# mLSTM exponents as full-height products with zeros for the other direction, and float32r tiles moved in SBUF

## The chip, the cores and the metric

The kernel runs on one core of one Trainium2 chip. Its time is measured on the device, in microseconds (us): before the change the median of three runs is 1986.36 us, from 1985.49 to 1988.99. TensorE (PE) multiplies matrices; each product is a weight load (PEld) and a stream of the other operand, the moving one, past the loaded weights. VectorE (DVE) and ScalarE (ACT) do elementwise work, GpSimd (POOL) sets memory and does a little arithmetic, SyncE (SP) issues transfers. On-chip memory has 128 partitions; an address is a byte offset that is the same in every partition.

## The reference

Two layers (DEPTH = 2) over 512 latent and 256 context tokens of width 1024. Each layer: a modulated RMSNorm, one projection `w_in`, four mixers side by side (gated DeltaNet, windowed attention, spatial gating, bidirectional mLSTM), one projection `w_out`, then an MLP of width 4096. The part of the mLSTM that the change touches is this, for each direction, head and chunk:

```
b    = cumsum(log_sigmoid(f));  dmat[i,j] = b[i] - b[j] + ig[j]   (j <= i, else -inf)
m[i] = max(b[i] + m_prev, max_j dmat[i,j])
s    = (q k^T) * exp(dmat - m)        # the exponents
h    = (exp(b + m_prev - m) * (q C) + s v) / max(|den|, exp(-m))
```

The second direction runs over reversed tokens, and both directions' outputs are added.

## The kernel before, in words

Activations lie transposed, 128 features on the partitions and up to 768 tokens along each. A float32 product is made of three float32r products: both operands are split into a rounded high part and a rest, and `gemm` (L484) adds `whi x hhi`, `whi x hlo`, `wlo x hhi` for each of eight blocks of 128 rows. Weights come by DMA into `wst`, ACT writes the high part `whi`, DVE the rest `wlo` (`wsplit`, L456). Two halves of a weight block take turns over the buffers that `wset` lists: in the output projection and the MLP six pairs, four of them in the pool `wcp` and two in `wsp`, so that two of three gemms read their weights from `wcp`. The activations are the moving operand: 512 latent tokens and, in layer 0, also 256 context tokens, thus 24 products of 512 columns for each gemm (and 24 of 256 in layer 0). The output projection and the MLP are 72 gemms for each layer.

Pools are laid one behind the other in SBUF, and a tile's address follows from the sizes of what lies ahead of it. In the program before the change the tiles of the gemms start at these distances past a multiple of 128 bytes (rows of weights and segments of tokens are whole multiples of 512 bytes, so that every slice keeps its tile's distance):

| tile | used as | bytes past a multiple of 128 |
|---|---|---|
| `hhi`, `hlo`, `mhi`, `mlo`, `fhi`, `flo` | moving operand of all gemms | 64 |
| `whi`, `wlo` in `wsp` | weights | 64 |
| `whi`, `wlo` in `wcp`, layer 0 | weights | 32 |
| `whi`, `wlo` in `wcp`, layer 1 | weights | 96 |
| `whi`, `wlo` in the DeltaNet's `Y1`, `Nh` | weights | 32 |
| `khi`, `klo` of head pair 0, `qs` | attention scores | 32 |
| `La`, `Rm` | the mLSTM's exponents | 32, 96 |
| `ident_r`, `gmask_r`, `selP_r`, `sel2_r` | constants | 96 |

The mLSTM's exponents are made in `mlstm_weights` (L1398), for each block p of 128 tokens. Rows 0 to 15 of `La` and `Rm` belong to the forward direction, rows 32 to 47 to the backward one. One DVE instruction (L1402) writes `Rm` for both directions: minus the running maximum, copied to four heads by the mask `d4p`. Then, in a loop over the directions, a product of 16 rows `La x Rm` (tile `W`) and a bfloat16 product that adds the triangular mask (L1414, L1415), ACT's exponential, DVE's multiplication with `qks`, and the decay `qw` towards the state (`wexp`). `Rm` has two buffers.

All of this, the attention (`swa`) and four dense projections stand in one block for each layer (L1488) that is scheduled by a simulation of its instructions, so that the order on each engine is its choice. Elsewhere the order is the scheduler's too, under the waits that buffers set.

Of the kernel before, what the change touches and what calls it, by code (L numbers as in the profile page):

```python
# [9 lines left out]
F32 = mybir.dt.float32  # L10
F32R = mybir.dt.float32r
F16 = mybir.dt.float16
BF16 = mybir.dt.bfloat16
AF = mybir.ActivationFunctionType
# [7 lines left out]
NT = SEQ + CTX  # L22
# [21 lines left out]
def go(t):  # L44
# [2 lines left out]

_LAYOUT = (
    ("ident", 128), ("blk64", 128), ("triA", 128), ("triB", 128), ("fwd", 128), ("rev", 128), ("rot", 128),
    ("d4", 4), ("d4p", 4), ("nlo", 2), ("csel", 8), ("sgn", 32), ("eps", 1), ("odg", 64), ("half", 2),  # L50
    ("gmask", 128), ("up", 128), ("lw", 128), ("selP", 128), ("sel2", 256), ("lvl", 384),
    ("cos", 512), ("sin", 512),
)
# [10 lines left out]
def constants():  # L64

    c = np.zeros((128, NCONST), np.float32)

    def put(name, a):
        o, w = _OFF[name]
        c[:a.shape[0], o:o + w] = a  # L70

    p = np.arange(128)
    same = (p[:, None] // 64) == (p[None] // 64)
    le = p[:, None] <= p[None]
    ge = p[:, None] >= p[None]
    lo_half = p < 64
    put("ident", np.eye(128))
    put("blk64", same)
    put("triA", same & np.where(lo_half[None], le, ge))
    put("triB", same & np.where(lo_half[None], ge, le))  # L80
    put("fwd", le)
    put("rev", ge)
    rot = np.zeros((128, 128))
    for h in range(2):
        for i in range(32):
            rot[64 * h + 32 + i, 64 * h + i] = -1.0
            rot[64 * h + i, 64 * h + 32 + i] = 1.0
    put("rot", rot)
    t = np.arange(SEQ)
    inv = np.power(np.float32(10000.0), -np.arange(16, dtype=np.float32) / np.float32(16)).astype(np.float32)  # L90
    ang = np.concatenate([(t // 64).astype(np.float32)[:, None] * inv, (t % 64).astype(np.float32)[:, None] * inv], 1)
    ang = np.tile(ang.astype(np.float64).T, (4, 1))
    put("cos", np.cos(ang))
    put("sin", np.sin(ang))
    g = np.zeros((128, 2, 64))
    j, i = p[:, None] % 64, np.arange(64)[None]
    for s in range(2):
        d = (p[:, None] >= 64) ^ bool(s)
        ok = np.where(d, i <= j, i >= j)
        g[:, s] = np.where(ok, 0.0, NEG)  # L100
    put("gmask", g.reshape(128, 128))
    put("up", np.where(p[None] >= p[:, None], 0.0, NEG))
    put("lw", np.where(p[None] <= p[:, None], 0.0, NEG))
    r = np.arange(64)
    half, k8 = r // 32, r % 32
    live = k8 < 8
    put("selP", live[:, None] & ((p[None] >= 64) == half[:, None]))
    sel2 = np.zeros((64, 2, 128))
    for q in range(2):
        sel2[:, q] = live[:, None] & ((r[:, None] % 4) == 2 * q + (p[None] >= 64))  # L110
    put("sel2", np.tile(sel2.reshape(64, 256), (2, 1)))
    put("d4", live[:, None] & ((r[:, None] % 4) == np.arange(4)[None]))
    put("d4p", (k8 < 16)[:, None] & ((r[:, None] % 4) == np.array([0, 2, 1, 3])[None]))
    put("nlo", np.where(np.stack([k8 // 4 == 1, k8 // 4 == 3], 1), -1.0, 0.0))
    lv = [np.where((j // 2 == i // 2) & (j != i), -1.0 / 1024.0, 0.0)]
    for n in range(1, 6):
        b = 1 << n
        lv.append(((j // (2 * b) == i // (2 * b)) & (j // b != i // b)) / 1024.0)
    put("lvl", np.concatenate(lv, 1))
    cs = np.zeros((128, 8))  # L120
    for k in range(4):
        cs[32 * k, 2 * k] = cs[32 * k + 1, 2 * k + 1] = 1.0
    put("csel", cs)
    sg = np.ones((128, 32))
    sg[:, 8:16] = sg[:, 24:32] = -1.0
    put("sgn", sg)
    put("eps", np.full((128, 1), EPS))
    put("half", np.stack([lo_half, ~lo_half], 1))
    put("odg", np.where(j == i, 0.0, 1024.0))
    return c  # L130


def bc(ap, axis, n):
    shape = list(ap.shape)
    shape.insert(axis, n)
    return ap.unsqueeze(axis).to_broadcast(shape)
# [3 lines left out]
def flow_kernel(ctx, tc, t, out, dbg=None, stop=None):  # L140
    nc = tc.nc
    V, S, T, G = nc.vector, nc.scalar, nc.tensor, nc.gpsimd
# [3 lines left out]
    per = ctx.enter_context(tc.tile_pool(name="per", bufs=1))  # L146
# [5 lines left out]
    pps = ctx.enter_context(tc.tile_pool(name="pps", bufs=4, space=PSUM))  # L152
    pg = ctx.enter_context(tc.tile_pool(name="pg", bufs=1, space=PSUM))

    S.preload_act_table_set("natural_log_exp_and_others")

    def ps(name="ps", dt=F32):
# [15 lines left out]
    def mm(o, l, r, start=True, stop=True):  # L173
        T.matmul(o, lhsT=l, rhs=r, start=start, stop=stop)  # L174

    def act_(o, i, f, **kw):
        S.activation(out=o, in_=i, func=f, **kw)  # L177

    def tt(o, a, b, op, eng=None):
        (eng or V).tensor_tensor(out=o, in0=a, in1=b, op=op)  # L180

    def stt(o, a, s, b, op0, op1):
        V.scalar_tensor_tensor(out=o, in0=a, scalar=s, in1=b, op0=op0, op1=op1)  # L183

    MUL, ADD, SUB, MAX, MIN = ALU.mult, ALU.add, ALU.subtract, ALU.max, ALU.min


    crow = per.tile([16, 128], F32, name="crow")
    nc.sync.dma_start(out=crow, in_=t["crow"])

# [4 lines left out]
    def cc(name):  # L195
        o, w = _OFF[name]
        return cst[:, o:o + w]

    ident, blk64, eps, odg = cc("ident"), cc("blk64"), cc("eps"), cc("odg")
    nlo, nlo_a = (cc("nlo")[0:64, i:i + 1] for i in range(2))  # L200
    d4, d4p = cc("d4")[0:64], cc("d4p")[0:64]
    ones = const.tile([128, 128], F32, name="ones")
    V.memset(ones, 1.0)
    scT = per.tile([128, 8, 32], F32, name="scT")
# [78 lines left out]

    def layer_pools():
        lay = ctx.enter_context(ExitStack())
        return lay, lay.enter_context(tc.tile_pool(name="zp", bufs=1)), lay.enter_context(tc.tile_pool(name="ta", bufs=2))

    lay, zp, tp = layer_pools()
    ldx = ExitStack()
    ld = ldx.enter_context(tc.tile_pool(name="ld", bufs=5))  # L290

    sg = per.tile([128, 16], F32, name="csg")
    cv = per.tile([128, 16], F32, name="cv")
    pt = gi("cT")
    T.transpose(pt[:, 0:16], crow, ident[0:16, 0:16])
    V.tensor_copy(out=cv, in_=pt[:, 0:16])
# [292 lines left out]
    for l in range(DEPTH):  # L589
# [13 lines left out]
        if l:  # L603
            lay, zp, tp = layer_pools()
# [8 lines left out]
        h = modulated(l, 0, ALL, nrm, tp)  # L613
# [10 lines left out]
        o, o_k0 = gemm_pair(ahead, h, ALL, (32, 128))  # L624
        evac(zg[0:32], o, ALL, 32)
        o = ps("gatesT")
# [49 lines left out]
        for i, (which, j) in enumerate(((0, 0), (2, 0), (0, 1), (2, 1), (1, 0), (1, 1))):  # L676
            qlat = which == 1 and last
            segs = LAT if qlat else ALL
            o = gemm(None, h, segs, w2=ready.pop(i)) if i else o_k0
# [29 lines left out]
        for s_, d_ in ((0, 0), (0, 1), (1, 0), (1, 1)):  # L709
            d = s_ ^ d_  # L710
# [6 lines left out]
        o = ps("gc")  # L717
# [22 lines left out]
        for f in range(2):  # L740
            o = ps("glps")
# [290 lines left out]
        o = ps("wsT")  # L1032
# [100 lines left out]
        bl = zp.tile([64, 6], F32, name="bl")  # L1133
        V.tensor_copy(out=bl, in_=o[0:64, 0:12:2])

        La = sw1.tile([64, NT], F32R, name="La")
        hi = tp.tile([128, GAP + 4], F32R, tag="tb", name="rhi")[0:64, 0:NT]
        act_(hi, aR, AF.Copy)
        stt(La, hi.bitcast(F32), nlo_a, aR, MUL, ADD)
# [258 lines left out]
        def mlstm_weights(p):  # L1398

            pc = slice(128 * p, 128 * p + 128)  # L1400
            R = ml2.tile([64, 4, 128], F32R, tag="Rm", name="Rm")
            stt(R, bc(Mhl[:, pc].bitcast(F32), 1, 4), -1.0, bc(d4p, 2, 128), MUL, MUL)  # L1402
            qks = ml2.tile([128, 512], F32, tag="qks", name="qks", bufs=1)
            for r in range(2):
                o = (gi, go1)[r]("qk")
                hp = slice(64 * r, 64 * r + 64)
                for q in range(2):
                    mm(o[:, 128 * q:128 * q + 128], lk[q][hp, pc], lq[q][hp, pc])
                act_(qks[:, 256 * r:256 * r + 256], o[:, 0:256], AF.Copy, scale=0.125)
            res = []  # L1410
            for d in range(2):
                o = (gi, go1)[d]("W")
                rp = slice(32 * d, 32 * d + 16)
                mm(o, La[rp, pc], R[rp].rearrange("p h i -> p (h i)"), True, False)  # L1414
                mm(o.rearrange("p (h i) -> p h i", h=4), ident_b, bc((up_b, lw_b)[d], 1, 4), False, True)  # L1415
                sT = ml2.tile([128, 512], F32, tag="sT", name="sT", bufs=4)
                act_(sT, o, AF.Exp)
                tt(sT, qks, sT, MUL)
                qw = None
                if p != (0, 1)[d]:  # L1420
                    qw = ml2.tile([128, 2, 128], F32, tag="qw", name="qw", bufs=4)
                    wexp(d, p, qw)
                    for j in range(2):
                        stt(qw[:, j], lq[j][:, pc], 0.125, qw[:, j], MUL, MUL)
                res.append((sT, qw))
            return p, res
# [80 lines left out]

        pc_ = ctx.enter_context(ExitStack())
        hid_p = pc_.enter_context(tc.tile_pool(name="hid", bufs=8))
        tp = pc_.enter_context(tc.tile_pool(name="tc", bufs=2))  # L1510
        adp = pc_.enter_context(tc.tile_pool(name="adp", bufs=2))
        wcp = pc_.enter_context(tc.tile_pool(name="wcp", bufs=2))
        wset[:] = [(wcp, "whi", "wlo")] * 2 + [(wcp, "whi2", "wlo2")] * 2 + [(wsp, "whi", "wlo")] * 2
        mh = []
        for j in MIXK:
# [96 lines left out]
```

## Time and profile before

| what | us |
|---|---|
| median of three runs | 1986.36 |
| profiled execution | 1991.04 |
| its span, first to last instruction | 1989.3 |
| PE busy in it | 1911.8 |
| DVE busy | 1193.3 |
| ACT busy | 755.6 |

Around the span lie 1.7 us. A busy PE is not PE at its peak: a product's own duration (0.39 us for 512 columns) covers its way through the array, and the next one starts while it is under way. What a product costs in a row of products is therefore the distance from its start to the next start, read from the timeline. The mean granted clock of TensorE over the span is 0.968 of full speed.

### The profile page before, as it was taken

The page shows a single profiled execution, that of the slowest core. Times are in us where ns is not written, and L with a number is a line of the kernel's source. Part 1 is how long each engine was busy: PE and PEld are TensorE (multiplying, and loading weights), DVE is VectorE, ACT ScalarE, POOL GpSimd, SP SyncE. Part 2 cuts the span into 40 slices and gives each one's busy share as a digit, 9 for nine tenths or more (in the row PEclk, how much of TensorE's full clock was granted, in tenths as well). Part 3 has the DMA queues.
Part 4 walks back from the last instruction along what each step waited for, and adds up shares of the span by engine and source line. Part 5 has one row for each costly group of instructions (what it writes and reads, how often), then busy time and mean ns, then how long its engine had stood idle before and what let it go on. Part 6 is the DMA issues. An engine that isn't in the chain of part 4 may idle for free.

```text
span 1989.3 us, 33924 instructions
## 1 busy us (share of the span) xinstructions
PE 1911.8 (96%) x14107; PEld 1552.5 (78%) x14107; DVE 1193.3 (60%) x2200; ACT 755.6 (38%) x1528; POOL 100.1 (5%) x161
## 2 busy tenths in 40 slices
PE   5999999999999999999999999999999999999998
PEld 3877778777777888888888878677777778888887
DVE  3978785555769556435534459788766654444343
ACT  4652233444524312213213237334255543333242
POOL 0021110000000000000000000212000000000001
PEclk7999999898799999999999999999999999999999
DMA  8220001121374344334433212210011323333332
GB/s 310 87 58 27 13 15 42 55 64 33 110 219 129 105 138 138 118 95 148 140 94 96 78 53 59 57 34 23 23 43 33 106 74 96 96 95 96 96 95 74
DMA packets 225633, 172.27 MB, mean 87 GB/s; under 512 B 19042, under 2 KB 207816, under 8 KB 225480
## 3 DMA queue, kind: packets, MB, share of 16 engines
q1 hardware_dynamic: 219104, 153.38, 26.2%
q10 hardware_dynamic: 4680, 10.70, 1.5%
q0 software_dynamic: 1696, 6.03, 0.9%
q8 instruction: 110, 1.80, 0.4%
q14 instruction: 43, 0.35, 0.1%
HBM read 162.75 MB, written 7.34 MB: 86 GB/s over the span
## 4 chain that ended last, share of the span: by engine, by line
PE 84%; DVE 7%; ACT 4%; DMA 3%; issue 1%; POOL 0%; SPq 0%; ACTq 0%; DVEq 0%
PE mm L174 64%; PE mmt L174 3%; DMA wst<-w_in 1%; PE num L174 1%; PE ops L174 1%; PE pv L174 1%; PE pT L1329 1%; DVE Y L180 1%; PE yt L174 1%; PE t L174 1%; PE adaps L174 1%; PE Eps L174 1%; DVE kq L183 1%; PE scl L174 1%; PE yps L174 1%
## 5 line engine op out<-in xcount | busy, mean ns | idle before, releaser
L177 ACT ACTIVATE whi<-wst 128x512 fp32r<-128x512 f32 (+1 forms) x388 | 242.0, 627 | 700.4 <-PE mm L174 636.0
L174 PE MATMUL mm<-hhi,whi 128*128 128x512 f32 (+3 forms) x1344 | 480.6, 363 | 12.0 <-ACT hhi L177 10.7
L174 PE MATMUL mm<-hlo,whi 128*128 128x512 f32 (+3 forms) x1344 | 482.1, 359 | 1.4 <-DVE hlo L183 1.2
L174 PE MATMUL mm<-hhi,wlo 128*128 128x512 f32 (+3 forms) x1344 | 477.7, 358 | 0.1
L180 DVE TENSOR_TENSOR wlo<-wst,whi 128x512 fp32r<-128x512 f32 (+1 forms) x388 | 265.2, 687 | 327.5 <-ACT whi L177 321.1
L174 PEld LDWEIGHTS mm<-hhi,whi 128*128 128x128 f32 (+1 forms) x1344 | 252.7, 189 | 56.6 <-ACT hhi L177 14.2
L174 PEld LDWEIGHTS mm<-hlo,whi 128*128 128x128 f32 (+1 forms) x1344 | 253.6, 189 | 41.4 <-DVE hlo L183 2.9
L174 PEld LDWEIGHTS mm<-hhi,wlo 128*128 128x128 f32 (+1 forms) x1344 | 253.0, 189 | 41.2 <-issue 2.7
L174 PE MATMUL mm<-flo,whi 128*128 128x512 f32 (+1 forms) x784 | 277.8, 354 | 0.0
L174 PE MATMUL mm<-fhi,whi 128*128 128x512 f32 (+1 forms) x784 | 277.2, 354 | 0.0
L174 PE MATMUL mm<-fhi,wlo 128*128 128x512 f32 (+1 forms) x784 | 275.9, 352 | 0.0
L174 PEld LDWEIGHTS mm<-fhi,whi 128*128 128x128 f32 x784 | 147.7, 188 | 24.1 <-ACT r L177 0.8
L183 DVE SCALAR_TENSOR_TENSOR x<-mm,mod,x 128x256 f32<-128x256 f32 (+1 forms) x122 | 79.6, 653 | 142.0 <-PE mm L174 141.8
L174 PEld LDWEIGHTS mm<-fhi,wlo 128*128 128x128 f32 x784 | 147.6, 188 | 21.5
L174 PEld LDWEIGHTS mm<-flo,whi 128*128 128x128 f32 x784 | 147.8, 189 | 21.2
L183 DVE SCALAR_TENSOR_TENSOR adacc<-adw,scT,adacc 128x1024 f32<-128x1024 f32 x84 | 105.7, 1280 | 28.8 <-DMA adw<-ada_w 28.4
L180 DVE TENSOR_TENSOR flo<-r,fhi 128x768 fp32r<-128x768 f32 (+1 forms) x64 | 52.5, 824 | 39.1 <-ACT fhi L177 39.0
L174 PE MATMUL mm<-mlo,whi 128*128 128x512 f32 (+1 forms) x192 | 71.3, 372 | 0.8 <-DVE mlo L180 0.8
L174 PE MATMUL mm<-mhi,whi 128*128 128x512 f32 (+1 forms) x192 | 71.0, 370 | 1.0 <-ACT mhi L177 1.0
L177 ACT ACTIVATE fhi<-r 128x768 fp32r<-128x768 f32 (+1 forms) x64 | 47.2, 739 | 64.9 <-DVE r L180 64.9
L174 PE MATMUL mm<-mhi,wlo 128*128 128x512 f32 (+1 forms) x192 | 70.2, 365 | 0.0
L177 ACT ACTIVATE r<-mm 128x256 f32<-128x256 f32 (+1 forms) x96 | 49.2, 516 | 32.2 <-PE mm L174 32.2
(403 smaller groups left out, 2734.0 us busy)
## 6 DMA issues: line engine op xcount, KB each, us to landing
wst<-mlp_w SPq DMA_DIRECT2D x128, 512.0 KB, 4.2
adw<-ada_w SPq DMA_DIRECT2D x96, 512.0 KB, 4.3
wst<-w_in SPq DMA_DIRECT2D x44, 512.0 KB, 3.9
wst<-w_out SPq DMA_DIRECT2D x64, 128.0 KB, 3.2
xd<-x ACTq DMA_DIRECT2D x8, 384.0 KB, 3.6
x<-xd POOLq DMA_DIRECT2D x8, 384.0 KB, 7.7
xs<-x ACTq DMA_DIRECT2D x4, 512.0 KB, 7.4
wst<-w_in SPq DMA_DIRECT2D x8, 256.0 KB, 3.7
```

The costliest lines, as they stand in the source:

```text
L174: T.matmul(o, lhsT=l, rhs=r, start=start, stop=stop)
L177: S.activation(out=o, in_=i, func=f, **kw)
L180: (eng or V).tensor_tensor(out=o, in0=a, in1=b, op=op)
L183: V.scalar_tensor_tensor(out=o, in0=a, scalar=s, in1=b, op0=op0, op1=op1)
L1329: T.transpose(o[:, 256 * i + 128 * g:256 * i + 128 * g + 128], Ps[g][:, 128 * (i0 + i):128 * (i0 + i) + 128], ident)
```

## The change

Exponents. `Rm` becomes two tiles of 128 rows, one for each direction, each with one buffer. The new mask `d4q` holds in its first four columns the heads of the forward direction, with zeros on all other rows, and in its last four those of the backward one. `Lw` is `La` with 64 more rows, which GpSimd sets to zero (the rows 64 to 127 of `MD`, which the DVE instruction now reads too, hold other finite numbers, and the mask's zeros take them away). Each direction's product then runs over all 128 rows. The decays (`wexp`, `qw`) of both directions follow in a loop of their own behind the exponents of both.

Places. `lead` puts 32 bytes ahead of the pools `per` and `zp`; two small tiles leave `per`; `d4q` is 16 bytes longer than `d4p`; `wcp` moves ahead of the pools `tc` and `adp`. After that the tiles of the table start at 0 past a multiple of 128, all but `Rm` (64) and the second head pair's `klo` (32, before 64); `MD` goes from 64 to 32.

```diff
@@ -47,7 +47,7 @@
 
 _LAYOUT = (
     ("ident", 128), ("blk64", 128), ("triA", 128), ("triB", 128), ("fwd", 128), ("rev", 128), ("rot", 128),
-    ("d4", 4), ("d4p", 4), ("nlo", 2), ("csel", 8), ("sgn", 32), ("eps", 1), ("odg", 64), ("half", 2),
+    ("d4", 4), ("d4q", 8), ("nlo", 2), ("csel", 8), ("sgn", 32), ("eps", 1), ("odg", 64), ("half", 2),
     ("gmask", 128), ("up", 128), ("lw", 128), ("selP", 128), ("sel2", 256), ("lvl", 384),
     ("cos", 512), ("sin", 512),
 )
@@ -110,7 +110,8 @@
         sel2[:, q] = live[:, None] & ((r[:, None] % 4) == 2 * q + (p[None] >= 64))
     put("sel2", np.tile(sel2.reshape(64, 256), (2, 1)))
     put("d4", live[:, None] & ((r[:, None] % 4) == np.arange(4)[None]))
-    put("d4p", (k8 < 16)[:, None] & ((r[:, None] % 4) == np.array([0, 2, 1, 3])[None]))
+    put("d4q", (k8 < 16)[:, None] & (half[:, None] == np.arange(8)[None] // 4)
+        & ((r[:, None] % 4) == np.array([0, 2, 1, 3] * 2)[None]))
     put("nlo", np.where(np.stack([k8 // 4 == 1, k8 // 4 == 3], 1), -1.0, 0.0))
     lv = [np.where((j // 2 == i // 2) & (j != i), -1.0 / 1024.0, 0.0)]
     for n in range(1, 6):
@@ -152,6 +153,10 @@
     pps = ctx.enter_context(tc.tile_pool(name="pps", bufs=4, space=PSUM))
     pg = ctx.enter_context(tc.tile_pool(name="pg", bufs=1, space=PSUM))
 
+    def lead(pool, n):
+
+        pool.tile([128, n // 4], F32, tag="lead", name="lead", bufs=1)
+
     S.preload_act_table_set("natural_log_exp_and_others")
 
     def ps(name="ps", dt=F32):
@@ -185,6 +190,7 @@
     MUL, ADD, SUB, MAX, MIN = ALU.mult, ALU.add, ALU.subtract, ALU.max, ALU.min
 
 
+    lead(per, 32)
     crow = per.tile([16, 128], F32, name="crow")
     nc.sync.dma_start(out=crow, in_=t["crow"])
 
@@ -198,7 +204,7 @@
 
     ident, blk64, eps, odg = cc("ident"), cc("blk64"), cc("eps"), cc("odg")
     nlo, nlo_a = (cc("nlo")[0:64, i:i + 1] for i in range(2))
-    d4, d4p = cc("d4")[0:64], cc("d4p")[0:64]
+    d4, d4q = cc("d4")[0:64], cc("d4q")
     ones = const.tile([128, 128], F32, name="ones")
     V.memset(ones, 1.0)
     scT = per.tile([128, 8, 32], F32, name="scT")
@@ -283,14 +289,16 @@
 
     def layer_pools():
         lay = ctx.enter_context(ExitStack())
-        return lay, lay.enter_context(tc.tile_pool(name="zp", bufs=1)), lay.enter_context(tc.tile_pool(name="ta", bufs=2))
+        z, t_ = lay.enter_context(tc.tile_pool(name="zp", bufs=1)), lay.enter_context(tc.tile_pool(name="ta", bufs=2))
+        lead(z, 32)
+        return lay, z, t_
 
     lay, zp, tp = layer_pools()
     ldx = ExitStack()
     ld = ldx.enter_context(tc.tile_pool(name="ld", bufs=5))
 
-    sg = per.tile([128, 16], F32, name="csg")
-    cv = per.tile([128, 16], F32, name="cv")
+    sg = ld.tile([128, 16], F32, name="csg", bufs=1)
+    cv = ld.tile([128, 16], F32, name="cv", bufs=1)
     pt = gi("cT")
     T.transpose(pt[:, 0:16], crow, ident[0:16, 0:16])
     V.tensor_copy(out=cv, in_=pt[:, 0:16])
@@ -1133,7 +1141,10 @@
         bl = zp.tile([64, 6], F32, name="bl")
         V.tensor_copy(out=bl, in_=o[0:64, 0:12:2])
 
-        La = sw1.tile([64, NT], F32R, name="La")
+
+        Lw = sw1.tile([128, NT], F32R, name="La")
+        La = Lw[0:64]
+        G.memset(Lw[64:128].bitcast(F32), 0.0)
         hi = tp.tile([128, GAP + 4], F32R, tag="tb", name="rhi")[0:64, 0:NT]
         act_(hi, aR, AF.Copy)
         stt(La, hi.bitcast(F32), nlo_a, aR, MUL, ADD)
@@ -1398,8 +1409,9 @@
         def mlstm_weights(p):
 
             pc = slice(128 * p, 128 * p + 128)
-            R = ml2.tile([64, 4, 128], F32R, tag="Rm", name="Rm")
-            stt(R, bc(Mhl[:, pc].bitcast(F32), 1, 4), -1.0, bc(d4p, 2, 128), MUL, MUL)
+            R = [ml2.tile([128, 4, 128], F32R, tag=f"Rm{d}", name="Rm", bufs=1) for d in range(2)]
+            for d in range(2):
+                stt(R[d], bc(MD[:, pc].bitcast(F32), 1, 4), -1.0, bc(d4q[:, 4 * d:4 * d + 4], 2, 128), MUL, MUL)
             qks = ml2.tile([128, 512], F32, tag="qks", name="qks", bufs=1)
             for r in range(2):
                 o = (gi, go1)[r]("qk")
@@ -1407,16 +1419,16 @@
                 for q in range(2):
                     mm(o[:, 128 * q:128 * q + 128], lk[q][hp, pc], lq[q][hp, pc])
                 act_(qks[:, 256 * r:256 * r + 256], o[:, 0:256], AF.Copy, scale=0.125)
-            res = []
+            sTs, res = [], []
             for d in range(2):
                 o = (gi, go1)[d]("W")
-                rp = slice(32 * d, 32 * d + 16)
-                mm(o, La[rp, pc], R[rp].rearrange("p h i -> p (h i)"), True, False)
+                mm(o, Lw[:, pc], R[d].rearrange("p h i -> p (h i)"), True, False)
                 mm(o.rearrange("p (h i) -> p h i", h=4), ident_b, bc((up_b, lw_b)[d], 1, 4), False, True)
-                sT = ml2.tile([128, 512], F32, tag="sT", name="sT", bufs=4)
-                act_(sT, o, AF.Exp)
-                tt(sT, qks, sT, MUL)
-                qw = None
+                sTs.append(ml2.tile([128, 512], F32, tag="sT", name="sT", bufs=4))
+                act_(sTs[d], o, AF.Exp)
+                tt(sTs[d], qks, sTs[d], MUL)
+            for d in range(2):
+                sT, qw = sTs[d], None
                 if p != (0, 1)[d]:
                     qw = ml2.tile([128, 2, 128], F32, tag="qw", name="qw", bufs=4)
                     wexp(d, p, qw)
@@ -1507,9 +1519,9 @@
 
         pc_ = ctx.enter_context(ExitStack())
         hid_p = pc_.enter_context(tc.tile_pool(name="hid", bufs=8))
+        wcp = pc_.enter_context(tc.tile_pool(name="wcp", bufs=2))
         tp = pc_.enter_context(tc.tile_pool(name="tc", bufs=2))
         adp = pc_.enter_context(tc.tile_pool(name="adp", bufs=2))
-        wcp = pc_.enter_context(tc.tile_pool(name="wcp", bufs=2))
         wset[:] = [(wcp, "whi", "wlo")] * 2 + [(wcp, "whi2", "wlo2")] * 2 + [(wsp, "whi", "wlo")] * 2
         mh = []
         for j in MIXK:
```

The change moves instructions in the scheduled block. The first place is DVE in layer 0's block, around the exponents of the second and third token block (`Rm` above; `den`, `hn`, `hs`, `ss` are the mLSTM's output sum, `P` and `sm` the attention's softmax). Before:

```order
L1315 RECIPROCAL sm<-sm 128x2
L180 TENSOR_TENSOR sT<-qks,sT 128x512
L1318 TENSOR_SCALAR P<-P,sm 128x640 x2
L1458 TENSOR_REDUCE ss<-sq_5285 128x4
L180 TENSOR_TENSOR hs<-hs,ss 128x256
L183 SCALAR_TENSOR_TENSOR Rm<-MD,cst 64x512
L279 TENSOR_SCALAR ta<-ta 128x768
```

And now:

```order
L1462 RECIPROCAL den<-den 128x8
L188 SCALAR_TENSOR_TENSOR Rm<-MD,cst 128x512
L185 TENSOR_TENSOR hn<-num,den 128x512
L185 TENSOR_TENSOR sm<-sm 128x2
L185 TENSOR_TENSOR hs<-hn 128x256
L185 TENSOR_TENSOR sT<-qks,sT 128x512
L185 TENSOR_TENSOR sm<-sm 128x2
L1470 TENSOR_REDUCE ss<-sq_5292 128x4
L1326 RECIPROCAL sm<-sm 128x2
L1329 TENSOR_SCALAR P<-P,sm 128x640 x2
L185 TENSOR_TENSOR hs<-hs,ss 128x256
L188 SCALAR_TENSOR_TENSOR Rm<-MD,cst 128x512
```

Where one instruction wrote both directions' `Rm`, two stand now, one for each direction, at places of their own.

The second place is PE in the same block, behind a dense projection (`mm`): `wps` is the decay's product, `pT` and `num` belong to the attention and the output sum. Before:

```order
L174 MATMUL mm<-hhi,wlo 128x512
L174 MATMUL wps<-MD,sel_r 128x128 x2
L174 MATMUL W<-Rm,La 128x512
L174 LDWEIGHTS ident_b
L174 MATMUL W<-lw_b,ident_b 128x512
L1329 MATMUL pT<-cst,P 128x128 x4
```

And now:

```order
L179 MATMUL mm<-hhi,wlo 128x512
L179 MATMUL W<-Rm,La 128x512
L179 LDWEIGHTS ident_b
L179 MATMUL W<-lw_b,ident_b 128x512
L179 MATMUL wps<-MD,sel_r 128x128 x2
L1340 MATMUL pT<-cst,P 128x128 x4
```

The backward direction's exponents now stand ahead of the decay's product, and the product and its mask still follow each other.

The third place is SP at the start of layer 0's output projection (`wst` are weights, `adw` the blocks of the modulation's matrix). Before:

```order
L358 DMA adw<-ada_w 128x1024 x2
L478 DMA wst<-w_out 128x2x128 x4
L358 DMA adw<-ada_w 128x1024
L478 DMA wst<-w_out 128x2x128 x4
L358 DMA adw<-ada_w 128x1024
```

And now:

```order
L366 DMA adw<-ada_w 128x1024 x2
L486 DMA wst<-w_out 128x2x128 x7
L366 DMA adw<-ada_w 128x1024
L486 DMA wst<-w_out 128x2x128
L366 DMA adw<-ada_w 128x1024
```

Three of the four transfers of one weight block move ahead of one modulation block; elsewhere SP's order is the same.

## Rows read from the trace of the kernel before

**Rows 1.** The page: busy time, share of the span, instructions.

```profile
PE 1911.8 (96%) x14107; PEld 1552.5 (78%) x14107; DVE 1193.3 (60%) x2200; ACT 755.6 (38%) x1528; POOL 100.1 (5%) x161
```

**Rows 2.** The page: chain that ended last, shares of the span by engine and line.

```profile
PE 84%; DVE 7%; ACT 4%; DMA 3%; issue 1%; POOL 0%; SPq 0%; ACTq 0%; DVEq 0%
PE mm L174 64%; PE mmt L174 3%; DMA wst<-w_in 1%; PE num L174 1%; PE ops L174 1%; PE pv L174 1%; PE pT L1329 1%; DVE Y L180 1%; PE yt L174 1%; PE t L174 1%; PE adaps L174 1%; PE Eps L174 1%; DVE kq L183 1%; PE scl L174 1%; PE yps L174 1%
```

**Rows 3.** Groups by shape: names, rows*columns, moving operand, count | busy us, mean ns | idle.

```profile
L174 PE MATMUL mm<-hhi,whi 128*128 128x512 f32 x832 | 334.5, 404 | 3.4 <-ACT hhi L177 3.0 <-ACT P L177 0.3
...
L174 PE MATMUL mm<-fhi,whi 128*128 128x512 f32 x496 | 195.3, 394 | 0.0
...
L174 PE MATMUL mm<-hhi,whi 128*128 128x256 f32 x480 | 139.1, 291 | 2.7 <-ACT hhi L177 1.8 <-ACT vt L177 0.7 <-PE glps L174 0.2
...
L174 PE MATMUL mm<-fhi,whi 128*128 128x256 f32 x288 | 81.9, 284 | 0.0
...
L174 PE MATMUL mmt<-whi,hhi 128*128 128x256 f32 x176 | 54.5, 310 | 0.0
```

**Rows 4.** PE's timeline, layer 1's MLP: start, duration (us); weights at 96, from 1810.57 at 64.

```profile
1799.38 0.39 PE L174 MATMUL mm<-hhi,whi 128*128 128x512 f32 x1
...
1808.48 0.39 PE L174 MATMUL mm<-hhi,whi 128*128 128x512 f32 x1
...
1812.65 0.39 PE L174 MATMUL mm<-hhi,whi 128*128 128x512 f32 x1
...
1815.37 0.39 PE L174 MATMUL mm<-hhi,whi 128*128 128x512 f32 x1
```

**Rows 5.** PE's timeline, layer 0's MLP: weights at 32, from 706.78 at 64.

```profile
702.55 0.28 PE L174 MATMUL mm<-fhi,whi 128*128 128x256 f32 x1
...
703.98 0.39 PE L174 MATMUL mm<-fhi,whi 128*128 128x512 f32 x1
...
706.78 0.28 PE L174 MATMUL mm<-fhi,whi 128*128 128x256 f32 x1
...
708.21 0.40 PE L174 MATMUL mm<-fhi,whi 128*128 128x512 f32 x1
...
710.96 0.28 PE L174 MATMUL mm<-fhi,whi 128*128 128x256 f32 x1
```

**Rows 6.** PE's timeline in the DeltaNet: each value of clo is repeated over 64 columns.

```profile
1269.39 0.38 PE L174 MATMUL Eps<-clo,ident_r 128*128 128x512 f32 x1
1269.61 0.39 PE L174 MATMUL Eps<-gmask_r,ident_r 128*128 128x512 f32 x1
```

**Rows 7.** PE's timeline, the exponents of one token block in layer 0.

```profile
391.04 0.50 PE L174 MATMUL W<-Rm,La 16*128 16x512 f32 x1
391.47 0.39 PE L174 MATMUL W<-up_b,ident_b 128*128 128x512 bf16 x1
391.79 0.50 PE L174 MATMUL W<-Rm,La 16*128 16x512 f32 x1
```

**Rows 8.** The tile Rm: count, duration min/median/max, starts; then idle time before it.

```profile
L183 DVE SCALAR_TENSOR_TENSOR Rm<-MD,cst x10: 674/682/685, 351.0 to 1498.9; 64x512 fp32r<-64x512 f32 x10
its engine sat idle before it (us, times) until:
  PE W L174: 7.6, 3
```

**Rows 9.** Stretches: us, busy PE, PEld, DVE, ACT, POOL, granted clock, DMA.

```profile
345.00:530.00 185.00, 172.29 (x1200) 138.04 (x1201) 108.38 (x301) 91.82 (x248) 0.00 (x0) 0.89 0.13 41
530.00:610.00 80.00, 78.00 (x473) 62.62 (x472) 56.04 (x75) 24.51 (x37) 4.35 (x8) 0.94 0.75 237
1430.00:1565.00 135.00, 127.78 (x870) 101.26 (x869) 91.23 (x246) 70.31 (x186) 0.00 (x0) 0.94 0.12 32
1640.00:1989.00 349.00, 343.77 (x1553) 280.44 (x1551) 149.77 (x226) 116.97 (x196) 9.16 (x7) 1.00 0.32 93
```

**Rows 10.** GpSimd's timeline before layer 0's block.

```profile
334.46 0.74 POOL L1145 MEMSET tc<- 64x768 f32 x1 [4.79 <-PE aRp L1128]
```

## The prediction

> **What bounds the kernel now.** I began with the page's busy times, where the reader sees TensorE at 96% of the span and no other engine above 60% [rows 1]. The chain of waits says the same of the path: 84% of it is PE, 64% the dense products `mm` alone, 7% DVE [rows 2]. So whatever alters the pace of one dense product alters the time nearly one for one, and DVE counts only where PE waits for it. The groups by shape give the quantities: each row shown has two more like it (high by high, high by rest, rest by high), thus (832 + 496) x 3 = 3984 products of 512 columns and (480 + 288 + 176) x 3 = 2832 of 256 [rows 3]. Their mean durations (404 ns, 291 ns) overlap the next product, so I read the pace from starts on PE's timeline. In layer 1's MLP, 39 products with weights 96 bytes past a multiple of 128 lie between 1799.38 and 1808.48: 9.10 / 39 = 233.3 ns each. Twelve with weights at 64 lie between 1812.65 and 1815.37: 226.7 ns each [rows 4]. Both groups read activations at 64. 512 columns at 2.4 GHz are 213.3 ns, so each product carries 13 to 20 ns that are not its columns, and the place of the weights sets part of it. In layer 0's MLP the 12 products of a group take 2.80 us with weights at 32 (from 703.98) and 2.75 us with weights at 64 (from 708.21), 233.3 against 229.2 ns; 256 columns take 1.43 / 12 = 119.2 ns in both [rows 5].
>
> **The change, part by part.**
>
> Dense products, places. The change takes activations from 64 to 0 and weights from 32, 64 and 96 to 0. No row of before has both at 0, so the price is bounded. The rows show a period of 64: weights at 32 and at 96 cost alike, 233.3 ns, those at 64 less. The reading nearest to them is that distance 0 behaves as 64 does. Then the two thirds of the output projection's and the MLP's gemms that read from `wcp` get the pace of the others: 72 gemms x 24 x 2/3 = 1152 products of 512 columns in each layer. Layer 1: 1152 x (233.3 - 226.7) = 7.6 us. Layer 0: 1152 x (233.3 - 229.2) = 4.7 us. Its products of 256 columns gain nothing, by the equal 119.2. The bound on the good side is that all excess goes, priced under the first rival; on the other side, that 0 is a bad place like 32 and 96: the third of these gemms that had 226.7 would lose 576 x 6.6 + 576 x 4.1 = 6.2 us, and the remaining 3984 - 2 x 1728 = 528 products of 512 columns up to 528 x 6.6 = 3.5 us: 10 us lost. I take 7.6 + 4.7 = 12.3 us.
>
> Exponents on PE. A 16-row product takes 0.43 us to the next start (391.04 to 391.47); its mask behind it 0.32 [rows 7]. A full-height product of the same 512 columns takes 0.23 [rows 4]. Ten tiles `Rm` [rows 8] make 20 such products: 20 x (0.43 - 0.23) = 4.0 us. The mask's excess over 0.23, 20 x 0.09 = 1.8 us, could go too if it comes from the change of height; the other bound is that nothing goes, because the 0.43 is the half clock of a stretch whose mean granted clock is 0.89 [rows 9]. I take 4.0. The Trainium skill speaks against this step: "TensorE: Matmul & The Clock Gate", section "Why this matters for your kernels", has a single product of 32 rows take as long as one of 128, and puts the gain of small ones in several running at once. By it `W` saves nothing and the sum below would be 4 us smaller. The trace disagrees so far: 0.43 against 0.23, and the two 16-row products stand 0.75 us apart, not side by side [rows 7].
>
> Exponents on DVE. One instruction of 0.68 us for 64 rows and 512 columns [rows 8] becomes two of 128 rows. By the nearest row each costs 0.68, as columns per row are unchanged, so 10 x 0.68 = 6.8 us are added; at most 20 x 0.68 = 13.6 if twice the rows cost twice. The block of layer 0 has DVE busy for 108 of 185 us, that of layer 1 for 91 of 135 [rows 9], and this room hides it; without that cover the loss is the 6.8. The decays go behind both exponents, which brings the second `W` forward by two short products and delays the first `qw` as much: 0, within 1 us either way per layer.
>
> GpSimd. Two memsets of 64 rows at about 0.74 us (the row of such a tile [rows 10]) fall where POOL does nothing for the following 185 us [rows 9]: 0, at worst 1.5 us ahead of the block.
>
> Weights' queue. Three `w_out` blocks pass one `adw` block in SP's order. That stretch moves 237 GB/s and leaves PE idle for 2.0 of 80 us [rows 9]. Three blocks of 0.13 MB are 0.39 MB / 237 GB/s = 1.7 us by which `adw` comes later: between -2.0 and +1.7, taken as 0, since the order only swaps who waits. The smaller moves (`Y1`, `Nh`, scores, constants) touch some hundred products of 256 columns, which showed no difference between 32 and 64: 0.
>
> Sum: 12.3 + 4.0 = 16.3 us. PE is busy in 93 to 98.5% of the stretches concerned [rows 9], so I count 95%: 15.5 us. From the profiled execution, 1989.3 of span and 1.7 around it, 1991.0 - 15.5 = 1975.5. That execution lies 4.7 above the median of 1986.4, so the median forecast is 1971. Its own range, 1961 to 1981, takes half the gain as missing, or the mask and the earlier projections as gaining too.
>
> **Rivals.**
>
> *All excess goes (far faster).* 226.7 ns is 544 cycles, 17 x 32, and 32 cycles are 128 bytes of float32: a row of 2048 bytes that starts 64 past a multiple of 128 touches 17 pieces of 128 bytes, from 0 only 16. For 256 columns, 120.0 ns would be 9 pieces for 8, near the 119.2. For it also speaks that a product whose moving values repeat, so that it reads few bytes, takes 1269.61 - 1269.39 = 0.22 us (216 ns unrounded) with the same 512 columns [rows 6]. Against it: a fixed cost of 13 ns for each product would show the same rows, and the period of 64 leaves no difference between 64 and 0. Price: about 233 - 216 = 16 ns x 3984 = 64 us, and 119.2 - 108 (half of 216) = 11 ns x 2832 = 31 us; of these 95 us some 90%, since the stretches below full clock have less of it: 85, with `W` 89. 1991 - 89 - 4.7 = 1897. If only the columns' own 213.3 and 106.7 stay it is some 15 us less, 1882. The Trainium skill's page "TensorE: Matmul & The Clock Gate", section "Back-to-back issue gap", gives N / 2.4 + 2.5 ns, 215.8 for 512 columns. The trace agrees for the repeated operand alone and shows 227 to 234 for the others.
>
> *The places do nothing.* The 7 ns between `wcp` and `wsp` may belong to their distance from the activations rather than to 32 or 96, and `W` may be hidden behind DVE. Then 1982 to 1987. Against it stand two layers in which `wcp` lies at different places and shows the same 233.3 [rows 4, 5].
>
> *DVE stalls on Rm (slower).* With one buffer for each direction, every `Rm` after a layer's first two must wait until the previous block's `W` was read: 16 waits, and behind each stands DVE's whole queue, `sT`, `sm`, `P`, for which ACT and PE wait. Before, three such waits cost 7.6 us, 2.5 each [rows 8]. All 16 like that are 40 us, with the added 6.8 47 us. It decides once more than 16 of these 47 us reach the path; with half of them there, 1971 + 24 = 1995, with all 2018. Against it: DVE has 77 and 44 us of room in the two blocks [rows 9], and the order can put an `Rm` behind its `W`.
>
> **How the numbers follow.** Forecast 0.42; all excess goes 0.33; nothing 0.11; DVE stalls 0.14. The range goes from the lower end of the first rival to the stall with half on the path: 1880 to 1995; both signs but for 0.14 are on the fast side, and the likeliest case alone is 1961 to 1981. A change of 0.2%, about 4 us, is the least that can be told from none. Faster by more: the first two cases, 0.75, less a 0.01 for losses that offset them: 0.74. Within 0.2%: 0.12. Slower: 0.14.
>
> **What would show it.** Right: 512-column products in layer 1's MLP at 226.7 ns in all gemms, in layer 0 at 229 with 256 columns still at 119; `W` at 0.23 to the next start; `Rm` at 0.68 each, with idle time before it no longer than before. The first rival shows as 216 and 108 in place of 227 and 119. If 233 stays with `wcp`, the second holds. If the blocks' PE time falls short of their length by 10 us more than before and DVE's idle time stands before `Rm`, the third does. The forecast is wrong above all if distance 0 differs from 64, for which I have no row.

## The result, and the profile after

The changed kernel takes 1962.85 us (four runs, 1960.3 to 1970.76) beside 1987.67 us for the kernel before: a ratio of 0.9871, 95% interval 0.9845 to 0.9897, thus 24.8 us less where 15.5 were forecast. The forecast time, 1971, lies 8 us above the measured one. The profiled execution is one of 1960.3 us; in the page of the profile, first busy times, then the chain of waits by engine, answering to [rows 1, 2]:

```profile
PE 1881.4 (96%) x14107; PEld 1539.8 (79%) x14107; DVE 1196.3 (61%) x2210; ACT 754.2 (39%) x1528; POOL 101.1 (5%) x163
...
PE 82%; DVE 10%; ACT 4%; DMA 3%; issue 1%; POOL 0%; DVEq 0%; ACTq 0%; SPq 0%; POOLq 0%
```

PE's busy time falls by 30.4 us and the span by 30.8: the time came from TensorE. (DVE's share of the chain rises from 7 to 10%; it is 9% with the places alone too, so it need not come from the longer `Rm`.) Where, a cut of the span at the first product of each stage shows. The windows are layer 0's scheduled block, layer 0's MLP, layer 1's block and layer 1's MLP; columns as in [rows 9]. Before:

```profile
369.20:530.90 161.70, 152.31 (x1083) 120.67 (x1081) 99.47 (x278) 83.41 (x225) 0.00 (x0) 0.91 0.13 41
618.20:1176.50 558.30, 554.77 (x3200) 478.49 (x3200) 285.20 (x377) 153.52 (x257) 1.46 (x4) 1.00 0.37 110
1453.00:1566.50 113.50, 107.76 (x751) 82.46 (x749) 79.67 (x224) 65.05 (x172) 0.00 (x0) 0.97 0.12 33
1618.60:1989.30 370.70, 365.15 (x1632) 297.57 (x1632) 164.31 (x248) 126.14 (x211) 9.16 (x7) 0.99 0.31 90
```

And after:

```profile
366.30:524.30 158.00, 148.59 (x1082) 118.27 (x1080) 101.95 (x284) 84.06 (x225) 0.00 (x0) 0.94 0.14 44
611.70:1166.10 554.40, 550.87 (x3200) 479.65 (x3200) 285.13 (x378) 153.21 (x257) 1.45 (x4) 1.00 0.37 111
1435.90:1544.30 108.40, 102.79 (x750) 80.08 (x748) 81.25 (x227) 64.24 (x172) 0.00 (x0) 1.00 0.13 35
1596.20:1958.50 362.30, 356.91 (x1632) 296.51 (x1632) 164.26 (x248) 126.13 (x211) 9.17 (x7) 0.99 0.31 92
```

The MLPs give 3.9 and 8.4 us at an unchanged clock. The blocks give 3.7 and 5.1, and there the granted clock has risen, from 0.91 to 0.94 and from 0.97 to 1.00. The remaining 9.7 us of the span are 2.9 in the stretch before layer 0's block and 6.7 in layer 1's DeltaNet (276.5 to 269.8, clock 0.96 to 0.99); a second profile of the changed kernel, below, does not have them.

PE's timeline in layer 1's MLP, 48 products apart (columns as in [rows 4]):

```profile
1700.05 0.39 PE L179 MATMUL mm<-hhi,whi 128*128 128x512 f32 x1
...
1710.93 0.39 PE L179 MATMUL mm<-hhi,whi 128*128 128x512 f32 x1
```

10.88 / 48 = 226.7 ns over gemms from all six buffers, where two thirds had 233.3 [rows 4]. In layer 0's MLP the 512-column products of those two thirds went from 234.0 to 229.0 ns, their 256-column products from 119.1 to 120.3 (means over the stage). `Rm` after the change, the view of the tile, then what its engine waited for:

```profile
L188 DVE SCALAR_TENSOR_TENSOR Rm<-MD,cst x20: 642/688/694, 349.9 to 1505.1; 128x512 fp32r<-128x512 f32 x20
...
  PE W L179: 11.2, 8
```

The doubled rows cost 0.688 us for 0.682 [rows 8]; DVE waits for `W` eight times, 11.2 us together, instead of three times and 7.6.

### The profile page after: what moved, and what is told of

It reads as the page before. It is cut to its first block, busy times and chain, and to the rows that moved or that the text cites. A ratio compares the mean times of both kernels' runs of the same rounds, so it can differ in the third digit from the quotient of the medians.

```text
span 1958.5 us, 33935 instructions
## 1 busy us (share of the span) xinstructions
PE 1881.4 (96%) x14107; PEld 1539.8 (79%) x14107; DVE 1196.3 (61%) x2210; ACT 754.2 (39%) x1528; POOL 101.1 (5%) x163
## 4 chain that ended last, share of the span: by engine, by line
PE 82%; DVE 10%; ACT 4%; DMA 3%; issue 1%; POOL 0%; DVEq 0%; ACTq 0%; SPq 0%; POOLq 0%
PE mm L179 63%; PE mmt L179 2%; PE num L179 1%; PE ops L179 1%; DVE kq L188 1%; DMA wst<-w_in 1%; PE pv L179 1%; DVE wlo L185 1%; PE yt L179 1%; DVE Y L185 1%; PE adaps L179 1%; PE pT L1340 1%; PE t L179 1%; PE Eps L179 1%; PE yps L179 1%
```

## The experiments

Pace below is the mean distance between starts of the 512-column products in layer 1's MLP, with waits left out. The code shows the lines that matter of each edit; `...` stands for lines left out.

**The exponents alone.** The change without `lead`, with `wcp` in its old place and 96 bytes ahead of the constants, so that each tile keeps its old distance:

```diff
-    lead(per, 32)
...
+    lead(const, 96)
...
```

> The exponents of the change alone; every float32r tile lies as before the change (activations 64, wcp 32 or 96, constants 96 past a multiple of 128; a small tile, crow, moves into a free buffer to make room). Theory: the two parts add up, and the measured 24.8 us are 12 from the places of the weights and the rest from the exponents with the clock in their blocks. Then 1988 - 9 = 1979, between 1975 and 1984, with 233 ns for each 512-column product whose weights are in wcp and 0.23 us for W. Rival: the exponents are hidden and all comes from the places: 1985 to 1989.

Measured: ratio 0.9969, interval 0.9951 to 0.9987, median 1984.6 beside 1990.0. Layer 1's MLP stays at 370.5 us, the blocks take 159.3 and 108.4, `W` 0.24 to 0.35 us to the next start in 19 of 20 cases. So this part of the change shortens layer 1's block by all of its 5.1 us. By the medians the whole is worth 5 to 6 us, less than the 9 expected, though the interval reaches from 3 to 10. Layer 1's DeltaNet took 270.2 us here and 270.1 in the run with the order of the decays below, which has 16-row products, but 278.6 in the second profile of the changed kernel: its gain above belongs to neither part.

**The places alone.** The change with the old exponents:

```diff
-            R = [ml2.tile([128, 4, 128], F32R, tag=f"Rm{d}", name="Rm", bufs=1) for d in range(2)]
+            R = ml2.tile([64, 4, 128], F32R, tag="Rm", name="Rm")
```

> The places of the change alone; the exponents are made as before, with 16-row products. Theory: 226.7 ns for each 512-column product in the MLPs, 0.43 us for W, 1988 - 13 = 1975, between 1971 and 1979. Rival (all from the places): 1963, as after the change.

Measured: 0.9924 (0.9907 to 0.9941), 1974.5 us. The MLPs take 554.5 and 362.3 us as in the changed kernel, the blocks 161.4 and 116.0. The theory holds, and the two parts are separate: 15.1 us by this ratio and 6.2 by the other, together 21.3, between the 24.8 us of the first measurement of the change and the 19.5 of the second.

**Everything 64 bytes further.** A tile of 64 bytes ahead of the constants:

```diff
...
+    lead(const, 64)
     ones = const.tile([128, 128], F32, name="ones")
```

> The changed kernel with every float32r tile 64 bytes further (activations, weights and constants at 64 past a multiple of 128 in place of 0; crow moves into a free buffer to make room). Theory, a period of 64: the same pace, 226.7 ns for 512 columns and 119 to 120 for 256, and the same time, within 0.3% of the changed kernel. Rival: 128 is the period that counts; then the pace is that of the rows of before with weights at 64 only by chance, some products become slower, and the time rises by 5 us or more.

Measured: 0.9920 (0.9898 to 0.9941), MLPs 554.7 and 362.3 us, pace 226.8 ns. The time lies 0.5% behind the first measurement of the changed kernel, outside the 0.3% expected, and 0.2% behind the second. In the MLPs, where the rival asked for slower products, the difference is 0.3 us at most, so multiples of 128 in themselves are worth nothing. I took it for the period of 64. It shows as well what the two kernels have in common: equal distances of both operands.

**Weights at 32 alone.**

```diff
+        lead(wcp, 32)
         tp = pc_.enter_context(tc.tile_pool(name="tc", bufs=2))
```

> The changed kernel with wcp alone moved by 32 bytes: the weights of two thirds of the gemms in the output projections and the MLPs at 32, all else at 0. Theory: the weights' place alone sets the pace, 233 ns for those products, 226.7 for the others; 1152 x 2 products at 4 to 6.6 ns more: 1963 + 12 = 1975. Rival: what counts is that both operands and the buffers are laid out as in the change (their distance from the activations or their pools' order); then 1963 and 227 ns everywhere.

Measured: 0.9948 (0.9929 to 0.9968), MLPs 557.8 and 368.7 us, 233.2 ns with weights at 32 and 227.7 with those left at 0. 3.4 + 6.4 = 9.8 us come back, most of the 12.3 that the places bring in the MLPs.

**Activations at 32.**

```diff
     lead(per, 32)
+    lead(hpool, 32)
+    lead(wsp, 96)
...
```

(and 32 ahead of the MLP's hidden tiles).

> The changed kernel with all activations of the dense products at 32 past a multiple of 128; wcp at 32 (two thirds of the MLPs' gemms), wsp at 0 (one third). Read from starts in layer 1's MLP. Theory, only the weights' place counts: 226.7 ns with weights at 0, 233 with weights at 32. Rival, each operand must lie at a multiple of 64: 233 or more in both. Rival, both must lie at the same distance: 227 with weights at 32 and 233 at 0.

Measured, one run (1986.5 us). In PE's timeline, 24 products from 1706.53 have weights from `wsp`, the next 48 from `wcp`:

```profile
1706.53 0.39 PE L179 MATMUL mm<-hhi,whi 128*128 128x512 f32 x1
...
1712.14 0.40 PE L179 MATMUL mm<-hhi,whi 128*128 128x512 f32 x1
...
1723.28 0.39 PE L179 MATMUL mm<-hhi,whi 128*128 128x512 f32 x1
```

With weights at 0: 5.61 / 24 = 233.8 ns. The theory that only the weights' place counts falls: it asked for 226.7. With weights at 32: 232.1 here, but 227.3 in the gemms that read the hidden tiles, equally at 32. The two differ in the 128 that I had not counted: past a multiple of 256, `hhi` lies at 32, the hidden tiles and `wcp` at 160, `wsp` at 128. The hidden tiles beside `wsp` had 233.0.

**Weights at 64 and 96.** A second pool for two of the pairs:

```diff
+        wcq = pc_.enter_context(tc.tile_pool(name="wcq", bufs=2))
+        lead(wcp, 64)
+        lead(wcq, 32)
...
```

> The changed kernel, activations at 0, with the MLPs' six weight buffers at three places: two pairs at 64, two at 96, two at 0. Theory, the weights alone with a period of 64: 226.7, 233 and 226.7 ns. Rival, same distance as the activations: 233, 233 and 226.7.

Measured, one run (1979.7 us): 233.3 ns at 64, 233.5 at 96, 228.5 at 0. Weights at 64 are bad when the activations are at 0 and were good when these were at 64 [rows 4]: the period of 64 falls, equal distance stands.

**Weights at 128 and 256.** The same kernel with leads of 128 and 128.

> The changed kernel with the MLPs' weight buffers at three places again: two pairs moved on by 128 bytes, two by 256, two left. In the changed kernel activations and these weights lie not only at 0 past a multiple of 128 but at 0 past a multiple of 512, the length of a weight row; so the earlier runs do not tell which distance repeats. Theory, equal distance past a multiple of 128 is enough: 227 ns in layer 1's MLP for all three. Rival, equal distance past a multiple of 512 counts: 233 ns for the weights at 128 and 256, 227 for those left, and 8 us more in layer 1's MLP.

Measured, one run (1973.4 us). Starts 24 products apart, weights in turn at 0, 128, 256:

```profile
1662.80 0.39 PE L179 MATMUL mm<-fhi,whi 128*128 128x512 f32 x1
...
1668.25 0.40 PE L179 MATMUL mm<-fhi,whi 128*128 128x512 f32 x1
...
1673.84 0.39 PE L179 MATMUL mm<-fhi,whi 128*128 128x512 f32 x1
...
1679.29 0.39 PE L179 MATMUL mm<-fhi,whi 128*128 128x512 f32 x1
```

5.45 / 24 = 227.1 ns at 0, 232.9 at 128, 227.1 at 256. Neither expectation holds: what repeats is 256. All the rows agree with one rule, equal distance past a multiple of 256: 0 and 0, 64 and 64, 160 and 160, and 192 and 192 (the exponents alone) are good; 64 beside 160 and 224 (before the change), 192 beside 32 and 96, 0 beside 32, 64, 96 and 128, 32 beside 128 and 160, and 160 beside 128 are bad. The change's multiples of 128 meet it because these tiles happen to lie at multiples of 512. The changed kernel has an exception that fits: the DeltaNet's `Y1` and `Nh` lie at 128 past a multiple of 256, and the 512-column products with these weights still have a median of 231 ns beside 227 for the others.

**Half the bytes.**

(The 512-column products read 256 tokens, each twice, and leave out the other 256.)

```diff
-                        mm(o[0:n, 0:cn], w[:, k, 0:n], a[:, c0:c0 + cn],
+                        mv = bc(a[:, c0:c0 + cn // 2], 2, 2) if cn == 512 else a[:, c0:c0 + cn]
...
```

> The changed kernel; in the dense products of 512 columns the moving operand is 256 values, each read twice in a row, so that a product of the same 512 columns reads half the bytes of a row (its result is that of the first 256 tokens twice; this part of the computation is changed). What are the 13 ns that stay beside 213.3? If they go with the bytes that the moving operand reads: 216 to 220 ns in place of 226.7, and some 4000 x 7 to 10 = 28 to 40 us less. If they are a fixed cost of each product: 226.7 and no change.

Measured, one run: 1927.3 us. PE's timeline in layer 1's MLP, 54 products apart:

```profile
1650.07 0.38 PE L179 MATMUL mm<-fhi,whi 128*128 128x512 f32 x1
...
1661.72 0.38 PE L179 MATMUL mm<-fhi,whi 128*128 128x512 f32 x1
```

11.65 / 54 = 215.7 ns: the 11 ns go when each value is read twice, so they are no fixed cost of a product. Whether it is the halved bytes or the repeating itself that saves them was not tried.

**The order of the decays.** The places alone, with the decays behind both exponents:

```diff
...
+                sTs.append(sT)
+            for d in range(2):
+                sT, qw = sTs[d], None
```

> The places of the change, the exponents as before (16-row products, one Rm of 64 rows with two buffers), but the decays of both directions behind both exponents as in the change. In the run of the places alone TensorE's clock fell in layer 1's scheduled block (0.94, 116.0 us) and does not fall in the kernels with full-height exponents (1.00, 108.4 us). Theory, the 16-row products bring the fall: it stays, 113 to 116 us. Rival, the order of the decays does it: 108 to 110 us at 1.00.

Layer 1's block in three kernels: the places alone, this one, and the exponents alone:

```profile
1445.20:1561.20 116.00, 110.28 (x751) 84.04 (x749) 79.68 (x224) 65.02 (x172) 0.00 (x0) 0.94 0.12 33
```

```profile
1450.80:1566.50 115.70, 109.94 (x750) 84.13 (x748) 79.69 (x224) 65.15 (x172) 0.00 (x0) 0.96 0.12 33
```

```profile
1443.80:1552.20 108.40, 102.70 (x751) 80.07 (x749) 81.35 (x227) 64.32 (x172) 0.00 (x0) 1.00 0.13 35
```

The theory's outcome, but the run does not separate what it was to separate. The edit moved the decays in the code, and the scheduler then made the same order of products on PE in layer 1's block as before, product for product in the trace. In the exponents alone, as in the changed kernel, about a quarter of the block's 750 products stand elsewhere. So the edit of the decays alone is excluded as a cause; full height and the new order on PE came together, and 16-row products in the new order were not tried.

**64 rows.**

```diff
-                mm(o, Lw[:, pc], R[d].rearrange("p h i -> p (h i)"), True, False)
+                mm(o, Lw[0:64, pc], R[d][0:64].rearrange("p h i -> p (h i)"), True, False)
```

> The changed kernel with the products W over the first 64 rows in place of 128 (their rows 64 to 127 hold zeros, the result is the same). Theory: fewer than 128 rows run at half pace whatever their number, 0.42 us to the next start, and the clock falls in layer 1's block as with 16 rows: 113 to 116 us there, and 5 to 8 us more in all than the changed kernel. Rival, only 16 or 32 rows are slow: 0.23 us, 108.4 us and the changed kernel's time.

Measured: 0.9932 (0.9913 to 0.9951), 1975.2 us beside 1968.2 for the changed kernel in the same runs. `W` takes 0.42 to 0.44 us to the next start in 16 of 20 cases, as with 16 rows. The order on PE in layer 1's block is that of the changed kernel. This block here, then in the kernel with weights at 128 and 256, which has full height:

```profile
1445.20:1556.30 111.10, 105.48 (x751) 81.24 (x749) 81.34 (x227) 64.34 (x172) 0.00 (x0) 0.98 0.12 34
```

```profile
1444.90:1555.60 110.70, 105.63 (x751) 82.24 (x749) 81.63 (x227) 64.31 (x172) 0.00 (x0) 0.97 0.13 34
```

The pace and the time of the whole are as expected, the fall of the clock is not: 111.1 us instead of 113 to 116, and at full height the clock fell as far or farther in this block in three of ten profiles (0.97 to 0.98). The slow product in the new order does not bring the old fall back, which speaks for the order rather than for the height; one profile does not decide it.

**The changed kernel again, and the DeltaNet's 64-row product full height too.**

> The changed kernel once more, to see how much of its 24.8 us is the run: by stages the places gave 12.2 us (3.8 and 8.4 in the two MLP stretches) and the exponents 5 in layer 1's block and 1 to 3 in layer 0's, 19 together, while 6.7 us in layer 1's DeltaNet came with a clock of 0.99 for 0.96 that other kernels also show by turns. Theory: 16 to 22 us below before, ratio 0.989 to 0.992. Rival, all 24.8 belong to the change: ratio 0.9871 again or below.

Measured: 0.9902 (0.9883 to 0.9921), 1968.2 beside 1989.2 us, 19.5 us by the ratio. In its profile the blocks take 157.9 and 108.4 us, the MLPs 554.7 and 362.3, but the stretch before the first block 371.4 and layer 1's DeltaNet 278.6 at 0.96. The four stages repeat, 3.8 + 3.6 + 5.1 + 8.4 = 20.9 us; the other 9.7 us of the first profile do not.

```diff
...
-            R = gd.tile([64, 2, 4, 64], F32R, tag="E", name="R")
+            R = gd.tile([128, 2, 4, 64], F32R, tag="E", name="R")
+            G.memset(R[64:128].bitcast(F32), 0.0)
...
```

> The changed kernel, and the DeltaNet's twelve 64-row products Eps (0.42 us to the next start) made full height in the same way, with rows 64 to 127 of R set to zero by GpSimd. Theory: 12 x (0.42 - 0.23) = 2.3 us less, and up to 8 more where the clock no longer falls in the DeltaNet; ratio to before 0.985 to 0.990. Rival: the memset of R, 0.5 to 0.7 us each, stands on the path ahead of Eps and gives back 12 x 0.6 = 7 us; then it is no faster than the changed kernel.

Measured: 0.9894 (0.9876 to 0.9913), 1967.6 us: beside 1968.2 not told apart from the changed kernel, so the theory's 2.3 us are not shown in the time. In the traces the product did get faster, 0.23 to 0.34 us to the next start in ten of twelve cases for 0.40 to 0.43 in the changed kernel, and the rival's reason is not there: the memsets take 0.52 us each, and PE waited for `R` 1.3 us in all, beside 2.0 in the changed kernel.

## Why the prediction was right or wrong

*Places, 12.3 us.* Right in size by luck, 3.9 + 8.4 = 12.3 us, and wrong in its reason. The step "the rows show a period of 64 [...] distance 0 behaves as 64 does" failed. It read the weights' place by itself, though the sentence before it said that both groups read activations at 64. What counts is the distance between the operands, past a multiple of 256; at 0 and 0 they agree as at 64 and 64, so the number came out. The bad case that I bounded at 10 us exists, but goes with unequal places: weights at 64 beside activations at 0 cost 6 ns a product. The agreement to the tenth is luck too. The term had 8 of 72 gemms in each output projection, 1.4 us, which do not show (87.3 us became 87.4 in layer 0, 52.1 became 51.9 in layer 1). In layer 0's MLP 1024 products gained 5.0 ns and 1024 of 256 columns, for which the term had nothing, lost 1.2: 5.1 - 1.2 = 3.9. In layer 1's, 1024 x (233.3 - 226.8) = 6.7 of the 8.4; the third that had equal places before also got 2 ns faster, some 1 us, and why is open.

Three counts of the prediction are wrong without touching its sum. Its 3984 products of 512 columns leave out those that read `mhi` and `mlo`, 384 (and 192 of 256 columns), while its 1728 for each layer hold them: the remaining 528 are 912, and the bad bound is 12 us. 233 - 216 is 17, not 16; with both, the first rival's 64 us are 74.

*Exponents on PE, 4.0 us.* This step failed: as a product's cost the term is mis-sized. In layer 1 before, PE's timeline around two of them:

```profile
1497.06 0.49 PE L174 MATMUL W<-Rm,La 16*128 16x512 f32 x1
1497.48 0.39 PE L174 MATMUL W<-lw_b,ident_b 128*128 128x512 bf16 x1
1497.80 0.66 PE L174 MATMUL num<-Cst,qw 64*128 64x66 f32 x4
```

And the same place after:

```profile
1479.89 0.50 PE L179 MATMUL W<-Rm,La 128*128 128x512 f32 x1
1480.23 0.39 PE L179 MATMUL W<-lw_b,ident_b 128*128 128x512 bf16 x1
1480.55 0.43 PE L179 MATMUL num<-Cst,qw 64*128 64x66 f32 x2
```

0.42 us became 0.34, not 0.23, and the mask keeps its 0.32: a dense run's pace does not hold beside products of 64 rows. Over all 20 the sum to the next start went from 7.5 to 6.2 us. Nor did all 20 take 0.43 before: in five cases the 16-row product ran beside the decay's two 32-row products, which use other rows. One of them, in layer 1:

```profile
1532.20 0.32 PE L174 MATMUL wps<-MD,sel_r 32*128 32x128 f32 x1
1532.21 0.50 PE L174 MATMUL W<-Rm,La 16*128 16x512 f32 x1
1532.37 0.27 PE L174 MATMUL wps<-MD,sel_r 32*128 32x128 f32 x1
```

Full height ends that: `W` and `wps` together cost 13.7 us before and 13.4 after, with waits left out. Of the 4.0 us, 0.3 came as the products' cost. The Trainium skill's rule that I weighed here ("TensorE: Matmul & The Clock Gate", section "Why this matters for your kernels") thus came nearer than my term: that small products gain by running at once shows in these five cases, which rows 7 alone did not show, while its equal time for one of them is not seen: 0.43 with 64 rows, 0.23 to 0.35 with 128.

Yet the blocks gained 8.8 us, most of it by the clock, which the prediction had only as a doubt about the 0.43. By an estimate from the granted clocks, layer 1's block ran 7 us at the half clock before and none after, which is worth 3.4 us, and layer 0's 29 and 19 us, worth 5. Two stretches of 4 us in layer 1's block before:

```profile
1496.50:1500.50 4.00, 4.00 (x24) 2.85 (x24) 1.59 (x8) 3.83 (x13) 0.00 (x0) 1.00 0.01 2
1500.50:1504.50 4.00, 4.00 (x24) 3.21 (x23) 4.00 (x12) 0.87 (x2) 0.00 (x0) 0.64 0.00 0
```

And after:

```profile
1479.30:1483.30 4.00, 4.00 (x26) 2.87 (x25) 2.51 (x8) 3.80 (x13) 0.00 (x0) 1.00 0.20 60
1483.30:1487.30 4.00, 4.00 (x28) 3.16 (x28) 4.00 (x13) 1.53 (x4) 0.00 (x0) 1.00 0.00 0
```

Before, PE was busy all through the first stretch, mostly with products of 64 and 16 rows, and then its clock fell to the half (0.64 is the mean over the 4 us). After, it did much the same work, in another order and with full-height `W`, and stayed at full clock. Layer 1's block took 113.5 to 116.0 us in all three profiles with 16 rows and 107.4 to 110.7 in all ten with full height. Layer 0's shows less: 161.2 to 161.7 against 157.8 to 161.4, so 0 to 4 us. That this part of the change brings the gain is shown, by the two parts run alone; whether the height of `W` or the order that came with it keeps the clock up stays open.

*DVE, hidden.* Right: 20 x 0.688 - 10 x 0.682 = 6.9 us more, and 3.6 us more of waiting, with PE's blocks shorter all the same. Only the sign that I gave, idle time before `Rm` no longer than before, did not hold. *GpSimd and SP, 0.* Right as far as it shows: the output projection of layer 0, before which the three transfers moved, takes 87.4 us for 87.3, and 88.9 in the second profile.

*The sum.* 15.5 against 24.8 us at first and 19.5 in the second measurement: the blocks gave some 5 us more than the term, and the first runs some 5 us that the second do not have.

*The rivals.* All excess goes: 226.7 stayed everywhere, so no; the 11 ns it was about do go when values are read twice, but not by alignment. By the Trainium skill ("TensorE: Matmul & The Clock Gate", section "Back-to-back issue gap") the estimate is 215.8 ns; the trace agrees only where values repeat (215.7). The places do nothing: excluded by the places alone. DVE stalls on `Rm`: the waits came, 11.2 us instead of the 40 of the price, and no loss from them shows: layer 1's block became 5.1 us shorter with them in it.

## What to carry to other kernels

Where a long run of float32r products is off its pace by some nanoseconds, compare the byte places of weights and moving operand with each other, not each with a round number, and try one kernel that moves one of them before padding everything. A term for a product's cost is to be read beside its own neighbours, all of them and not one row: a product of few rows can be slow in one place and run beside another elsewhere. Where the granted clock of a stage lies below 1, its fall can be worth more than the products counted. And where a scheduler sets the order, look in the trace whether an experiment on the order has changed it.

## What the runs showed of the hardware

- Weights and moving operand at equal distance past a multiple of 256 bytes: 227 ns for 512 float32r columns in layer 1's MLP (229 in layer 0's); at any other distance tried (multiples of 32): 231 to 234. For 256 columns unequal distances gave slightly less, 119.1 ns before against 120.3 after in layer 0's MLP.
- The 11 ns above 216 go when the moving operand's values are read twice each: 215.7 ns.
- A 512-column product of 16 or 64 rows takes 0.43 us to the start of a next one of 128 rows. Beside products of 32 rows on other rows, one of 16 rows ran at the same time: 0.01 and 0.16 us between the starts.
- TensorE's clock can fall to the half with the engine busy throughout: 4.00 of 4.00 us busy at 1.00, then 4.00 of 4.00 at a mean of 0.64.
- VectorE's `Rm` of 128 rows costs what the one of 64 does, 0.688 and 0.682 us.
